# Row sums of the mixing weights: from products with a matrix of ones to adding transfers in DRAM

## The chip, the cores and the metric

One Trainium2 chip, one of its cores. The metric is the device time of one execution in microseconds (us). The kernel before takes 894.17 us, the median of three runs (894.03 to 894.5).

## The reference

One layer on a sequence of 1024 tokens with 1024 channels. An input projection feeds two branches, attention and a gated MLP that mixes positions inside blocks of 128; the gated branches are summed, projected and added to the input. What matters here is the mixing:

```python
def chunked_spatial_gating(u, v, w_s, b_s, ln_g, ln_b):
    v = layernorm(v, ln_g, ln_b)
    vb = v.reshape(B, nb, SG_BLOCK, SG_GROUPS, SG_GROUP_WIDTH)
    mask = cidx[None, :] <= cidx[:, None]          # chunks of 64
    w = jnp.where(mask[None], w_s, 0)
    mixed = jnp.einsum('gij,bnjgc->bnigc', w, vb) + transpose(b_s)[None, None, :, :, None]
    return u * mixed.reshape(B, S, SG_WIDTH)
```

The gain `ln_g` and offset `ln_b` belong to a channel and the mixing sums over positions `j`, so the offset can be taken out of the sum: the mixed value is `ln_g * (w @ normalized v)` plus `ln_b` times the sum over `j` of `w[g, i, j]`, plus `b_s`. Those sums, 8 groups by 128 positions `i`, so 1024 numbers, are the row sums of this case. They are needed on all 128 partitions, because a partition holds a channel there.

## The kernel before, in words

All matmuls work on pairs of float32r parts: `split` (L169) makes a high part with a cast on ScalarE (L176) and a low part with a subtraction on VectorE (L177); the tiles have the tags `wh` and `wl`, three buffers each. A large product is done by seven partial products of quadrant sums (forms b11, t1, t2, b21, t3, b22, t4), each of them 12 matmuls on 512 columns.

The stage of the change has three stretches.

1. `late_product` (L1005) runs three times, for the forms t2, t3 and t4 of the MLP's values: two halves `c`, four token tiles `t` each, six matmuls for every step (L793). After each step `pace[0]` is its last matmul. After every odd `t` one of the prepared `early` transfers is issued (`part_of_early`): these are DRAM to DRAM transfers of 512 KB (L316) on the queue of GpSimd, which make weight sums that are first read at 557 us. `paced` makes a transfer wait for `pace[0]`.
2. Between the second and the third `late_product` stand four matmuls with a matrix of ones (L1059): the row sums come out of them, on all partitions, in two PSUM banks `ps_sc`. In front of them the masked mixing weights `mix_w` (tag `wT`, its masked quarter set to zero at L1046) are split like all other weights (L1048).
3. `gemm_pair` (L371) makes two rows of the U projection at a time, four times over (L1146). In each call seven products follow one another, with a `hook` after each. Here the hook is `both` (L1131): one early transfer, and then two items of the list `late`: eight `statistics_of`, `normalize`, `bias_of(0)`, and then the mixes that the `finish` functions append. With two items a hook, the first two mixes stand behind the sixth product of the first pair and the next two behind the seventh.

`bias_of` (L1092) works out bias + row sum * `ln_b` with four VectorE instructions for four groups (L1101). `mix` (L1108) does the mixing matmuls (L1112) into one of two PSUM banks `ps_tp`, scales and adds the bias (L1120), multiplies the U tile by the result (L1128) and stores it to `s1_dr` through SyncE's queue (L520). U tiles have the tag `x`, five buffers.

The order on each engine comes from a scheduler that takes, of the instructions that its model holds ready, the one that stands first in the program; `after(second, first)` forces an order on one engine without a wait, and a `Sync` dependency makes a real wait. Queues run in order: an instruction of SyncE or GpSimd that waits holds all that are behind it. Weight loads go through `copy_to` (L212) on SyncE.

Of the kernel before, what the change touches and what calls it, by code (L numbers as in the profile page):

```python
# [24 lines left out]
F32 = mybir.dt.float32  # L25
F32R = mybir.dt.float32r
AF = mybir.ActivationFunctionType
ALU = mybir.AluOpType
PSUM = bass.MemoryType.PSUM

P = 128
D = 1024
S = 1024
KC = D // P
HALF = 512
# [17 lines left out]
def hybrid_tile(  # L53
# [16 lines left out]
    nc = tc.nc  # L70
# [8 lines left out]
    def nm(s):  # L79
        count[0] += 1  # L80
        return f"{s}_{count[0]}"

    def bank(tag, dt=F32):
        return psum.tile([P, 512], dt, name=nm("ps_" + tag), tag="ps_" + tag, bufs=2)

    def mtile(shape, dt, tag, bufs, pool=None):
        return (pool or main).tile(shape, dt, name=nm(tag), tag=tag, bufs=bufs)

    def scratch(name, shape=(D, S)):
        return dram.tile(list(shape), F32, name=name)  # L90
# [4 lines left out]
    def xtile():  # L95
        return mtile([P, HALF], F32, "x", 5)


    def after(second, first):

        tc.add_manual_dep(
            second.ins,
            first.ins.name,
            mybir.DependencyInfo(mybir.DependencyClass.NoSync, mybir.DependencyReason.DATA),
            reason="order",
        )
# [6 lines left out]
    ident = const.tile([P, P], F32, name="ident")  # L113
# [15 lines left out]
    lb_sb = const.tile([P, KC], F32, name="lb_sb")  # L129
# [5 lines left out]
    k_dr = scratch("k_dr", (P, 4, S))  # L135
    v_dr = scratch("v_dr", (NT, P, 2, 3 * HD))
    s1_dr = scratch("s1_dr")
    z_dr = scratch("z_dr")
    gs_dr = scratch("gs_dr")
    ga_dr = scratch("ga_dr")  # L140
# [28 lines left out]
    def split(hi, lo, src, minus=False):  # L169
        if minus:  # L170
            hi_of.append(nc.scalar.mul(hi, src, -1.0))
            return nc.vector.scalar_tensor_tensor(
                lo, src, -1.0, hi.bitcast(F32), op0=ALU.mult, op1=ALU.subtract
            )
        else:
            hi_of.append(nc.scalar.copy(hi, src))  # L176
            lo_of.append(nc.vector.tensor_sub(lo, src, hi.bitcast(F32)))  # L177
            return lo_of[-1]
# [73 lines left out]
    def half_of(half):  # L252
        return slice(half * HALF, (half + 1) * HALF)
# [46 lines left out]
    def paced(move):  # L300

        if pace[0] is not None:
            tc.add_manual_dep(
                move.ins,
                pace[0].ins.name,
                mybir.DependencyInfo(mybir.DependencyClass.Sync, mybir.DependencyReason.DATA),
                reason="pace",
            )
# [41 lines left out]
    term = [None]  # L350
# [3 lines left out]
    def product(acc, part, form, fresh, last=True):  # L354
        wh, wl = part
        bh, bl = form
        for k in range(4):
            ks = slice(k * P, (k + 1) * P)
            for n, (lt, rt) in enumerate(
                ((wh[:, ks], bh[:, k, :]), (wh[:, ks], bl[:, k, :]), (wl[:, ks], bh[:, k, :]))  # L360
            ):
                nc.tensor.matmul(  # L362
                    acc,
                    lt,
                    rt,
                    start=fresh and k == 0 and n == 0,
                    stop=k == 3 and n == 2,
                    skip_group_check=True,
                )

    def gemm_pair(b, finish, hook=lambda: None, second="o"):  # L371

        n = done[0]
        done[0] += 1
        acc = bank("mm")[:]
        x11, x12, x22 = xtile(), xtile(), xtile()
        product(acc, ready[n, 0], b["b11"], True)
        pace[0] = nc.scalar.copy(x11[:], acc)  # L380
        hook()
        t5 = bank("o")[:]
        product(t5, ready[n, 2], b["t1"], True)
        pace[0] = nc.scalar.mul(x22[:], t5, -1.0)
        hook()
        product(acc, ready[n, 3], b["t2"], False)
        pace[0] = nc.scalar.copy(x12[:], acc)
        split_next()
        hook()
        t2 = bank(second)[:]  # L390
        product(t2, ready[n, 1], b["b21"], True)
        term[0] = term_of_x11[0] = nc.vector.tensor_add(x11[:], x11[:], t2)
        finish(0, 0, x11, x11[:], 1.0)
        split_next()
        hook()
        product(acc, ready[n, 4], b["t3"], False)
        term[0] = nc.vector.tensor_sub(x22[:], x22[:], acc)  # L397
        finish(1, 1, x22, x22[:], 1.0)
        hook()
        product(t5, ready[n, 5], b["b22"], False)  # L400
        term[0] = nc.vector.tensor_add(x12[:], x12[:], t5)
        finish(0, 1, x12, x12[:], 1.0)
        split_next()
        hook()
        product(acc, ready[n, 6], b["t4"], False)
        finish(1, 0, xtile(), acc, -1.0)
        split_next()
        hook()
# [102 lines left out]
    def part_of_early(every=2):  # L511
        hooks[0] += 1
        if early and hooks[0] % every == 0:
            early.pop(0)()
# [28 lines left out]
    pool = outer.enter_context(tc.tile_pool(name="mixing", bufs=1))  # L543
# [71 lines left out]
    casts, lows, turns, scalings, squares = [], [], [], [], []  # L615

    def add_on(dst, src):
        return nc.gpsimd.dma_start(dst, src, accum_op=ALU.add)
# [127 lines left out]
    def pair_of_w():  # L746
        return mtile([P, D], F32R, "wh", 3), mtile([P, D], F32R, "wl", 3)
# [220 lines left out]
    mix_w = mtile([P, KC, P], F32, "wT", 1, pool)  # L968
# [23 lines left out]
    def statistics(t, half):  # L992
        return nc.vector.bn_stats(stats[:, t, half, :], xh[:, t, half_of(half)])
# [5 lines left out]
            for i in range(2):  # L999
                after(statistics(t + i, 0), lows[-1])  # L1000

    ones = mtile([P, P], F32R, "ones", 1, pool)
    after(nc.vector.tensor_scalar(ones[:], ident[:], 0.0, 1.0, op0=ALU.mult, op1=ALU.add), lows[-1])

    def late_product(name, weight, done, aside):  # L1005
        for c in range(2):
            for t in range(4):
                pace[0] = vs_product(accs[t], name, t, weight, False, cs=(c,))
                if t % 2:
                    part_of_early(1)  # L1010
                if c:
                    done(t)
                if aside:
                    aside.pop(0)()
# [26 lines left out]
        + [lambda t=t: part_of("t3", t) for t in range(4)]  # L1041
        + [lambda: gelu_of(0), lambda: gelu_of(2)],
    )
    row_sums = [bank("sc") for half in range(2)]
    split_w("s3", 1)
    after(nc.vector.memset(mix_w[64:128, :, 0:64], 0.0), lows[-1])  # L1046
    wh, wl = pair_of_w()
    split(wh[:], wl[:], mix_w[:].rearrange("p g i -> p (g i)"))  # L1048
    late_product(
        "t3",  # L1050
        "s3",
# [2 lines left out]
        + [lambda t=t: part_of("t4", t) for t in range(4)]  # L1054
        + [lambda: split_w("a22", 0, a22[0][:]), lambda: gelu_of(4), lambda: gelu_of(6)],
    )
    for half in range(2):
        for n, part in enumerate((wh, wl)):
            nc.tensor.matmul(row_sums[half][:], ones[:], part[:, half_of(half)], start=n == 0, stop=n == 1)  # L1059
    split_w("a22", 1, a22[1][:])  # L1060
    part_of_early(1)
    begin_job()
# [8 lines left out]
    late = []  # L1071
    in_twos = set()

    def hook():
        if len(late) == 1 and late[0] in in_twos:
            return
        for _ in range(2):
            if late:
                late.pop(0)()

    def statistics_of(t):
        statistics(t, 1)
        nc.vector.bn_aggr(mv[:, t, :], stats[:, t])
# [8 lines left out]
    def bias_of(half):  # L1092

        wT = mix_w[:, half * 4 : half * 4 + 4, :]
        bg = first_bias
        if half:
            bg = mtile([P, 4, P], F32, "bias", 1, pool)
            nc.sync.dma_start(bg[:].rearrange("p g i -> p (g i)"), sg_b[half_of(half)].partition_broadcast(P))
        for gg in range(4):
            g = half * 4 + gg  # L1100
            nc.vector.scalar_tensor_tensor(  # L1101
                bg[:, gg, :], row_sums[half][:, gg * P : (gg + 1) * P], lb_sb[:, g : g + 1], bg[:, gg, :], op0=ALU.mult, op1=ALU.add
            )
        return bg, wT

# [25 lines left out]
    def both():  # L1131
        part_of_early(1)
        hook()

    late.extend(lambda t=t: statistics_of(t) for t in range(NT))
    late.append(normalize)
    for m in range(0, KC, 2):

        def finish(i, half, q, src, sign, m=m):
            nc.scalar.activation(q[:], src, AF.Gelu, scale=sign)  # L1140
            late.append(lambda: mix(m + i, half, q))
            in_twos.add(late[-1])

        if m % 4 == 0:
            late.append(lambda m=m: bias.append(bias_of(m // 4)))
        gemm_pair(hb, finish, both)  # L1146
    while late:
        late.pop(0)()
# [5 lines left out]
    pool = stage.enter_context(tc.tile_pool(name="keys", bufs=1))  # L1154
# [44 lines left out]
    pool = stage.enter_context(tc.tile_pool(name="queries", bufs=1))  # L1199
# [210 lines left out]
    pool = stage.enter_context(tc.tile_pool(name="attention", bufs=1))  # L1410
# [234 lines left out]
    pool = stage.enter_context(tc.tile_pool(name="later", bufs=1))  # L1645
# [384 lines left out]
    for p in range(4):  # L2030
        n, t, acc, x11 = N_PAIRS + p, T_ORDER[p], accs[p], firsts[p]
# [93 lines left out]
        for e in range(2):  # L2125
            cs = slice(e * wide, (e + 1) * wide)
            part = bank("sc")[:, 0:wide]
# [95 lines left out]
```

## Time and profile before

| | |
|---|---|
| median of three runs | 894.17 us |
| the profiled execution | 894.7 us |
| its span | 892.9 us |
| PE busy in the span | 881.7 us, 99% |
| VectorE busy | 684.9 us, 77% |
| ScalarE busy | 580.1 us, 65% |
| GpSimd busy | 150.9 us, 17% |
| DMA, read and written | 146.37 MB and 86.11 MB |

The profile shows one execution on the one core. Times in a row of the timeline are the start and the duration in us, counted from the span's start; the rest of the row is engine, line of the kernel, operation, and written tile `<-` read tiles. An arrow in brackets names what ended the engine's idle time before the row.

### The profile page before, as it was taken

The page shows a single profiled execution, that of the slowest core. Times are in us where ns is not written, and L with a number is a line of the kernel's source. Part 1 is how long each engine was busy: PE and PEld are TensorE (multiplying, and loading weights), DVE is VectorE, ACT ScalarE, POOL GpSimd, SP SyncE. Part 2 cuts the span into 40 slices and gives each one's busy share as a digit, 9 for nine tenths or more (in the row PEclk, how much of TensorE's full clock was granted, in tenths as well). Part 3 has the DMA queues.
Part 4 walks back from the last instruction along what each step waited for, and adds up shares of the span by engine and source line. Part 5 has one row for each costly group of instructions (what it writes and reads, how often), then busy time and mean ns, then how long its engine had stood idle before and what let it go on. Part 6 is the DMA issues. An engine that isn't in the chain of part 4 may idle for free.

```text
span 892.9 us, 13164 instructions
## 1 busy us (share of the span) xinstructions
PE 881.7 (99%) x4117; PEld 731.4 (82%) x4117; DVE 684.9 (77%) x1362; ACT 580.1 (65%) x1189; POOL 150.9 (17%) x217
## 2 busy tenths in 40 slices
PE   8999999999999999999999999999999999999996
PEld 6888888888888888888888888888888888888885
DVE  7979966566686778888878888847796578579886
ACT  6875533334445489989989899955685385467443
POOL 3322222203030001111211011101121121110012
PEclk9999999999999999999999999999999999999999
DMA  9998888958778667888786789989899789998533
GB/s 332 211 268 222 268 206 172 176 153 265 250 252 286 214 189 189 210 185 195 179 236 210 237 225 222 250 290 383 308 289 376 276 231 258 298 307 282 179 119 118
DMA packets 131410, 212.40 MB, mean 238 GB/s; under 512 B 12778, under 2 KB 59882, under 8 KB 131340
## 3 DMA queue, kind: packets, MB, share of 16 engines
q1 hardware_dynamic: 108808, 148.62, 50.0%
q0 software_dynamic: 22384, 62.67, 31.6%
q8 instruction: 33, 0.54, 0.2%
q14 instruction: 37, 0.30, 0.1%
q10 hardware_dynamic: 148, 0.27, 0.1%
HBM read 146.37 MB, written 86.11 MB: 260 GB/s over the span
## 4 chain that ended last, share of the span: by engine, by line
PE 92%; ACT 3%; DVE 2%; issue 1%; DMA 1%; POOL 0%; SPq 0%; ACTq 0%; DVEq 0%
PE ps_mm L362 42%; PE ps_o L362 24%; PE ps_tp L362 7%; PE ps_sc L362 3%; PE ps_tp L793 2%; PE ps_o L793 2%; PE ps_mm L793 2%; PE ps_tp L1515 2%; PE ps_sc L1442 2%; PE ps_tp L1112 2%; PE ps_o L1550 1%; PE ps_sc L793 1%; ACT wh L176 1%; DVE wl L177 1%; PE ps_o L1555 1%
## 5 line engine op out<-in xcount | busy, mean ns | idle before, releaser
L176 ACT CAST wh<-s 128x1024 fp32r<-128x1024 f32 (+1 forms) x79 | 79.4, 1006 | 75.2 <-PE ps_mm L362 23.5
L177 DVE TENSOR_TENSOR wl<-wr,wh 128x512 fp32r<-128x512 f32 (+1 forms) x77 | 72.0, 937 | 58.0 <-ACT wh L176 57.9
L177 DVE TENSOR_TENSOR wl<-s,wh 128x1024 fp32r<-128x1024 f32 (+1 forms) x79 | 92.9, 1176 | 11.8 <-ACT wh L176 11.7
L176 ACT CAST wh<-wr 128x512 fp32r<-128x512 f32 (+1 forms) x77 | 63.0, 819 | 55.9 <-PE ps_mm L362 31.5
L1448 ACT COPY sl<-ps_sc 128x384 f32<-128x384 f32 (+2 forms) x128 | 51.8, 456 | 9.9 <-DVE sm L1454 9.9
L362 PE MATMUL ps_o<-T_t1h,wh 128*128 128x512 f32 x148 | 57.9, 391 | 0.0
L362 PE MATMUL ps_o<-T_t1h,wl 128*128 128x512 f32 x148 | 57.7, 390 | 0.0
L362 PE MATMUL ps_o<-T_t1l,wh 128*128 128x512 f32 x148 | 57.6, 389 | 0.0
L1470 ACT ACTIVATE pr<-pr,sm 128x192 f32<-128x192 f32 (+2 forms) x128 | 56.2, 444 | 0.1
L1454 DVE CUSTOM_DVE_ANT_0 pr<-sl,nsink_sb 128x192 f32<-128x192 f32 (+2 forms) x128 | 48.0, 399 | 9.9 <-ACT sl L1448 8.8
L362 PE MATMUL ps_mm<-T_b11h,wh 128*128 128x512 f32 x140 | 54.9, 392 | 0.0
L362 PE MATMUL ps_mm<-T_t3h,wh 128*128 128x512 f32 x140 | 54.7, 390 | 0.0
L362 PE MATMUL ps_mm<-T_b11l,wh 128*128 128x512 f32 x140 | 54.6, 390 | 0.0
L362 PE MATMUL ps_mm<-T_t2h,wh 128*128 128x512 f32 x140 | 54.6, 390 | 0.0
L362 PE MATMUL ps_mm<-T_b11h,wl 128*128 128x512 f32 x140 | 54.6, 390 | 0.0
L362 PE MATMUL ps_mm<-T_t3h,wl 128*128 128x512 f32 x140 | 54.6, 390 | 0.0
L362 PE MATMUL ps_mm<-T_t2l,wh 128*128 128x512 f32 x140 | 54.6, 390 | 0.0
L362 PE MATMUL ps_mm<-T_t3l,wh 128*128 128x512 f32 x140 | 54.5, 390 | 0.0
L362 PE MATMUL ps_mm<-T_t2h,wl 128*128 128x512 f32 x140 | 54.5, 389 | 0.0
L362 PE MATMUL ps_mm<-T_t4h,wh 128*128 128x512 f32 x136 | 53.2, 391 | 0.3 <-DVE x L397 0.3
L362 PE MATMUL ps_mm<-T_t4h,wl 128*128 128x512 f32 x136 | 53.0, 390 | 0.0
L362 PE MATMUL ps_mm<-T_t4l,wh 128*128 128x512 f32 x136 | 52.9, 389 | 0.0
(432 smaller groups left out, 2448.5 us busy)
## 6 DMA issues: line engine op xcount, KB each, us to landing
wr<-in_w_dram SPq DMA_DIRECT2D x86, 256.0 KB
sums<-in_w_dram POOLq DMA_DIRECT2D x20, 512.0 KB, 7.0
s<-sums SPq DMA_DIRECT2D x20, 512.0 KB
q_hl<-qhl SPq DMA_DIRECT2D x16, 512.0 KB
q<-q_hl SPq DMA_DIRECT2D x64, 128.0 KB
y_dr<-x POOLq DMA_DIRECT2D x28, 256.0 KB, 6.8
g<-in_w_dram POOLq DMA_DIRECT2D x12, 512.0 KB, 6.8
wr<-in_w_dram SPq DMA_DIRECT2D x11, 512.0 KB
```

The lines of the kernel that those rows point to most:

```text
L176: hi_of.append(nc.scalar.copy(hi, src))
L177: lo_of.append(nc.vector.tensor_sub(lo, src, hi.bitcast(F32)))
L362: nc.tensor.matmul(acc, lt, rt, start=fresh and k == 0 and n == 0, stop=k == 3 and n == 2, skip_group_check=True,)
L793: mm = nc.tensor.matmul(acc[:], lt, rt, start=fresh and k == 0 and n == 0, stop=stops and k == 3 and n == terms[-1], skip_group_check=True,)
L1112: nc.tensor.matmul(pm[:, t * P : (t + 1) * P], xh[:, half * 4 + t, g * P : (g + 1) * P], bias[-1][1][:, g % 4, :], start=True, stop=True,)
L1442: nc.tensor.matmul(sc, q_of[:, c, i * P : (i + 1) * P], kt[:, :, lo:hi], start=True, stop=True)
L1448: copies.append(nc.scalar.copy(two, sc))
L1454: nc.vector.tensor_tensor_reduce(v, two[:, 0, :], two[:, 1, :], 1.0, nsk[:, i : i + 1], op0=ALU.add, op1=ALU.min, accum_out=nmax[:, c, i : ...
L1470: e = nc.scalar.activation(v, v, AF.Exp, bias=nmax[:, c, i : i + 1], scale=-1.0, accum_out=sums[:, c, i : i + 1])
L1515: nc.tensor.transpose(dst, pr[:, i, block * P : block * P + width], ident[:])
L1550: nc.tensor.matmul(po[:, first], va[1][:, vs], a[:, n, first], start=n == 0, stop=n == 1, skip_group_check=True)
L1555: nc.tensor.matmul(po[:, cs], vb[c][:, vs], b[c][:], start=t == 0, stop=True, skip_group_check=True)
```

## The change

The split of `mix_w`, the matrix of ones, the four matmuls and their two PSUM banks go. `mix_w` and its masked quarter stay, since the mixes read them. Instead a DRAM scratch `rs_dr` of 64 rows by 1024 is made:

- `first_rows` copies rows 0 to 63 of the weights (`j` as the row) into it, 256 KB, on SyncE's queue;
- `second_rows` adds rows 64 to 127 where the mask lets them through: 64 rows, 8 groups, runs of 64 numbers, on GpSimd's queue;
- `add_rows(n)` adds the lower `n` of the first `2n` rows onto the upper ones, for n = 32, 16, 8, 4, 2, 1;
- `load_row_sums(half)` loads half of row 0 into all 128 partitions of a tile `rs` (one buffer), on SyncE's queue.

All are `paced`. The steps take even `t` of the three `late_product` runs: `first_rows`, `second_rows`, and then every second place `add_rows(32)` to `add_rows(2)`. `add_rows(1)` and `load_row_sums(0)` become items of `late`, so that `normalize`, `bias_of(0)` and the mixes of the first pair come one hook later. `bias_of` now reads `rs` in SBUF instead of PSUM, and its four instructions are ordered behind the last addition of a product (`term[0]`).

```diff
+    rs_dr = scratch("rs_dr", (64, D))
...
-    ones = mtile([P, P], F32R, "ones", 1, pool)
-    after(nc.vector.tensor_scalar(ones[:], ident[:], 0.0, 1.0, op0=ALU.mult, op1=ALU.add), lows[-1])
+    def add_rows(n):
+        return lambda: paced(nc.gpsimd.dma_start(rs_dr[0:n], rs_dr[n : 2 * n], accum_op=ALU.add))
+
+    def first_rows():
+        paced(nc.sync.dma_start(rs_dr[:], sg_w[0:64].rearrange("j g i -> j (g i)")))
+
+    def second_rows():
+        paced(add_on(rs_dr[:].rearrange("j (g i) -> j g i", g=KC)[:, :, 64:P], sg_w[64:P, :, 64:P]))
+
+    def load_row_sums(half):
+        row_sums.append(mtile([P, HALF], F32, "rs", 1, pool))
+        paced(nc.sync.dma_start(row_sums[half][:], rs_dr[0][half_of(half)].partition_broadcast(P)))
+
+    row_sums = []
+    adding = [first_rows, second_rows]
+    for n in (32, 16, 8, 4, 2):
+        adding += [None, add_rows(n)]
...
                 if t % 2:
                     part_of_early(1)
+                elif adding:
+                    step = adding.pop(0)
+                    if step is not None:
+                        step()
...
-    row_sums = [bank("sc") for half in range(2)]
...
-    wh, wl = pair_of_w()
-    split(wh[:], wl[:], mix_w[:].rearrange("p g i -> p (g i)"))
...
-    for half in range(2):
-        for n, part in enumerate((wh, wl)):
-            nc.tensor.matmul(row_sums[half][:], ones[:], part[:, half_of(half)], start=n == 0, stop=n == 1)
...
-            nc.vector.scalar_tensor_tensor(
-                bg[:, gg, :], row_sums[half][:, gg * P : (gg + 1) * P], lb_sb[:, g : g + 1], bg[:, gg, :], op0=ALU.mult, op1=ALU.add
+            after(
+                nc.vector.scalar_tensor_tensor(
+                    bg[:, gg, :],
+                    row_sums[half][:, gg * P : (gg + 1) * P],
+                    lb_sb[:, g : g + 1],
+                    bg[:, gg, :],
+                    op0=ALU.mult,
+                    op1=ALU.add,
+                ),
+                term[0],
             )
...
+    late.append(add_rows(1))
     late.extend(lambda t=t: statistics_of(t) for t in range(NT))
+    late.insert(8, lambda: load_row_sums(0))
     late.append(normalize)
...
+        if m == 2:
+            late.append(lambda: load_row_sums(1))
```

More of the change, by code (lines that the diff above doesn't have):

```diff
@@ L1133, in both @@
         hook()
+    assert not adding
+    late.append(add_rows(1))
     late.extend(lambda t=t: statistics_of(t) for t in range(NT))
+    late.insert(8, lambda: load_row_sums(0))
     late.append(normalize)
```

## The prediction

> **What bounds the kernel now.** First the engines' shares on the page, then busy time by stretch around the change, then the chain that ended last.
>
> ```profile
> PE 881.7 (99%) x4117; PEld 731.4 (82%) x4117; DVE 684.9 (77%) x1362; ACT 580.1 (65%) x1189; POOL 150.9 (17%) x217
> ```
> ```profile
> core 0: us, PE busy (x) PEld busy (x) DVE busy (x) ACT busy (x) POOL busy (x), PEclk, DMA share, GB/s
> 50.00:82.20 32.20, 32.20 (x143) 26.64 (x142) 26.80 (x40) 22.50 (x32) 7.16 (x10) 1.00 0.93 233
> 83.40:110.00 26.60, 26.60 (x119) 22.04 (x118) 24.84 (x49) 14.06 (x19) 7.38 (x13) 1.00 0.87 267
> 305.00:450.00 145.00, 144.00 (x706) 120.52 (x705) 119.32 (x349) 127.98 (x365) 20.94 (x25) 1.00 0.79 195
> 450.00:610.00 160.00, 158.90 (x767) 132.24 (x767) 123.89 (x329) 135.94 (x350) 20.40 (x29) 1.00 0.82 244
> ```
> ```profile
> 79.89 2.72 PE ps_tp L793 x12
> 82.61 0.93 PE ps_sc L1059 x4
> 83.55 2.72 PE ps_mm L793 x12
> ...
> 108.03 2.73 PE ps_o L362 x12
> 110.75 1.78 PE ps_tp L1112 x16
> 112.54 2.78 PE ps_mm L362 x12
> 115.31 1.78 PE ps_tp L1112 x16
> 117.10 2.75 PE ps_mm L362 x12
> ```
>
> PE is the bound: full clock, no idle time in the stretches from 50 to 110 us, and the chain runs from matmul to matmul. The four products with ones stand on it for 0.93 us. The other thing to see is the DMA share of 0.93 and 0.87 in just those stretches: the new transfers go into engines that are nearly full.
>
> **What is removed.** On PE four matmuls, 0.93 us by the chain (0.23 us each; a product of 12 takes 2.72 us, the same rate). PE is busy on both sides without a gap, so this comes off whole: -0.93 us. On the other engines:
>
> ```profile
> 59.01 0.22 DVE L1003 TENSOR_SCALAR ones<-ident 128x128 fp32r<-128x128 f32 x1
> 74.43 1.04 ACT L176 CAST wh<-wT 128x1024 fp32r<-128x1024 f32 x1
> 75.92 1.22 DVE L177 TENSOR_TENSOR wl<-wT,wh 128x1024 fp32r<-128x1024 f32 x1
> ```
>
> 1.04 us of ScalarE and 1.44 us of VectorE go at a place where PE never waited for either, so I count them, and the freed pair of `wh` and `wl` buffers, at nothing: the weights merely get ready earlier. What is late next there is PE's own queue.
>
> **What is added: the chain of adds.** `first_rows`, `second_rows`, six adds and a load, each reading what the one before wrote, so each waits for its landing. Their places: `first_rows` behind the first step of the t2 run (the t2 and t3 runs are 8 x 2.72 = 21.8 us long and end at 82.6, so they begin at 60.8; 60.8 + 1.36 = 62.2 us), `second_rows` at 64.9, then adds at 70.4, 75.8, 81.3, 86.7 and 92.2 (four steps apart, 2 x 2.72 = 5.44 us; after 82.6 less 0.93), the last behind the first `x` copy of the pair. The nearest rows for their price:
>
> ```profile
> sums<-in_w_dram POOLq DMA_DIRECT2D x8, 512.0 KB, 6.9
> ```
> ```profile
> sums<-in_w_dram POOLq DMA_DIRECT2D x1, 512.0 KB, 4.1
> ```
> ```profile
> sums<-in_w_dram POOLq DMA_DIRECT2D x20, 256.0 KB, 8.3
> k_dr<-qhl POOLq DMA_DIRECT2D x16, 32.0 KB, 3.1
> ```
> ```profile
> 83.61 1.05 ACT L176 CAST wh<-wr 128x1024 fp32r<-128x1024 f32 x1
> ...
> 102.97 0.58 ACT L387 COPY x<-ps_mm 128x512 f32<-128x512 f32 x1
> ...
> 122.61 0.60 ACT L384 ACTIVATE x<-ps_o 128x512 f32<-128x512 f32 x1 [2.13 <-PE ps_o L362]
> 125.15 0.62 ACT L176 CAST wh<-wr 128x512 fp32r<-128x512 f32 x1 [1.94 <-PE ps_mm L362]
> 127.82 1.05 ACT L176 CAST wh<-wr 128x1024 fp32r<-128x1024 f32 x1 [1.57 <-PE ps_o L362]
> ```
> ```profile
> 111.08 0.68 DVE L401 TENSOR_TENSOR x<-x,ps_o 128x512 f32<-128x512 f32 x1
> 111.68 1.23 DVE L177 TENSOR_TENSOR wl<-s,wh 128x1024 fp32r<-128x1024 f32 x1
> 112.82 1.41 DVE L1120 SCALAR_TENSOR_TENSOR ps_tp<-ps_tp,lg_sb,bias 128x512 f32<-128x512 f32 x2
> 114.14 1.27 DVE L1128 TENSOR_TENSOR x<-x,ps_tp 128x512 f32<-128x512 f32 x2
> ...
> 145.11 1.12 DVE L1101 SCALAR_TENSOR_TENSOR bias<-ps_sc,lb_sb,bias 128x128 f32<-128x128 f32 x4 [2.42 <-DMA bias<-in_sg_b_dram]
> ```
> ```profile
> 104.23 0.80 SPq L212 DMA_DIRECT2D wr<-in_w_dram  x2
> 114.84 5.50 SPq L520 DMA_DIRECT2D s_dr<-x  x4
> 141.54 0.33 SPq L1098 DMA_DIRECT2D bias<-in_sg_b_dram  x1
> ...
> 557.48 1.23 SPq L212 DMA_DIRECT2D s<-sums  x2
> ```
>
> The DMA rows end with the median time from issue to landing: 6.9 us for the eight early transfers between 62 and 83 us, 4.1 us for the one issued at 100.8 us, 8.3 us for accumulating transfers of 256 KB, 3.1 us for small ones of 32 KB. No row shows a small DRAM accumulate in a full queue, so one add (T) lies between 3.1 and 8.3 us. I take 5.5: an add stands 1.36 us behind a 512 KB early transfer of the same queue that needs 6.9, so it lands about when that does, 6.9 - 1.36 = 5.5 us after its own issue; the 128 KB to 4 KB of its own are little. `second_rows` I take at 8.3, the dearest row, issued at 66 us (an estimate: `first_rows` lands 3.6 us after 62.2, like the load of the bias, which was issued at 141.54 and released VectorE at 145.11). It lands at 74.3; six adds in line bring 74.3 + 6 x 5.5 = 107.3; the load of half of row 0, repeated over the partitions like that of the bias, costs 3.6: the row sums are there at Z = 110.9 us. With T = 3.1 the places set the time: the load waits for the copy that ends at 103.55 - 0.93 = 102.6, so Z = 106.2. With T = 8.3, Z = 127.7.
>
> **When Z would cost something.** VectorE reads the row sums behind the addition of L401, which now ends at 111.76 - 0.93 = 110.8. From Z on: four bias instructions 1.12, two of L1120 1.41, the first of L1128 0.64, so the first mix's bank is free at Z + 3.2. PE needs that bank for the third mix. The mixes come one hook later: b22 ends at 110.75 - 0.93 = 109.8, t4 112.6, two mixes 114.4, b11 of the next pair 117.1, and there the third mix starts. So Z is free up to 113.9, costs one for one beyond, eats the gain at 114.8, and passes +0.2% at 116.6. By my Z of 110.9 the cost is 0, with 3 us of cover: the products between. That is T of 6.0, 6.15 and 6.45.
>
> **The other moved parts.** On GpSimd early transfers stand behind each waiting add; nothing reads their sums before 557 us. On SyncE `first_rows` holds the first weight loads of the pairs until 62.2, and their first cast is at 83.6; `load_row_sums(0)` holds the loads issued at 104.23, whose first cast comes at 127.8, and the stores of the mixes, which come at 116.7 (PE start of the first mix 112.6 plus the 4.1 between 110.75 and 114.84). Both queues are free by Z - 3.6 = 107.3. The stores free `x` buffers for the next pair: 116.7 and, taking the 4.1 to 8.3 us of the rows above, 120.8 to 125.0, against the copy at 122.61 - 0.93 = 121.7. ScalarE idles 1.94 us behind that copy and PE needs the x12 copy that follows only before t3, so some 3.5 us of delay are covered; 0, at worst a few tenths. `load_row_sums(1)` waits for nothing late: its sums are wanted at 145. The extra traffic, about 1.1 MB (256 + 128 + 252 + 512 KB), is 4.5 us of DMA at 250 GB/s; no load of this stretch is on PE's path.
>
> **Sum.** -0.93 + 0 = -0.93 us. Against the profiled execution, 894.7 us with its span of 892.9, that is 893.8 and 892.0; the median of the runs stands 0.5 below that execution, and from it, 894.17, the forecast is 893.2 us. A change of 0.2%, 1.8 us, is about what a measurement can tell from none, so this counts as the same.
>
> [...] The row gives 3.1 us for 32 KB and 8.3 for an accumulate of 256 KB. [...]
>
> **Rivals.**
>
> 1. *The chain comes late.* Each add waits behind the early transfers, and VectorE stands at the bias. For it: the DMA shares above and the 8.3 us row; against it: while GpSimd waits it issues no early transfers, and those from 86 us on land faster (4.1 us by 100.8). It decides from T = 6.15. Midway, at T = 6.8: Z = 118.7, stall 4.8, less 0.93: 898.0 us. At its end, T = 8.3: stall 13.8, 907.0 us.
> 2. *`second_rows` is slow by its form.* It moves 512 runs of 256 bytes; the trace has no accumulate in such runs, so 8.3 may be short. At twice that, 16.6, the rest as forecast: Z = 119.2, stall 5.3, 898.5 us. Only half of such a delay fits in the cover. [...]
> 3. *Faster beyond the four matmuls.* The scheduler lays out later stages anew. PE idles 1.0 us and 1.1 us in the two attention stretches of the table; half of these 2.1 us would give -2.0 and 892.2 us. Nothing in the profile speaks for that direction: those waits don't come from this stage.
> 4. *The change doesn't shorten PE* because something else held it there: PE shows no wait at 82 us, so I leave it inside the forecast's band (894.2, the same verdict).
>
> **Chances.** Forecast, with rival 4: 0.63 (892.8 to 894.3). Late chain: 0.20, since T needs to be only a tenth over my 5.5. `second_rows`: 0.05. Faster: 0.12. So faster 0.12, same 0.63, slower 0.25. The range runs from the faster case, 892.2, to the middle of the late one, 898.0; beyond lie about 0.06 below and 0.12 above.
>
> **What the profile after would show.** The chain passes from L793 to L793 at 82.6 without L1059. The adds on GpSimd's row each wait for the one before; `add_rows(1)` is issued near 102 us and the load on SyncE near 107. VectorE shows a wait for `rs` of at most a few us before four L1101-like rows, and PE none at 117. If the adds are later than 6.15 us apart, PE waits before the third mix, and the forecast is wrong by that wait.

## The result, and the profile after

The changed kernel takes 905.41 us (median of six runs, 902.24 to 908.25) against 894.29 us for six of the kernel before (893.72 to 895.34): a ratio of 1.0122, 95% interval 1.0107 to 1.0138. It is slower by 1.2%; the forecast was 893.2 us with a range up to 898.0.

The profiled execution is the shortest of the six, 902.24 us. Its page, and then from the summary of waits the rows of PE and VectorE that weren't there before (columns: who waits, for whom, us in total, times, longest):

```profile
span 900.3 us, 13176 instructions
PE 882.0 (98%) x4113; PEld 732.6 (81%) x4113; DVE 683.6 (76%) x1360; ACT 579.2 (64%) x1188; POOL 157.9 (18%) x224
PEclk9999989999999999999999999999999999999999
```
```profile
DVE bias L1116 <- DMA rs<-rs_dr: 8.4, 1, 8.4
PE ps_tp L1134 <- DVE x L1150: 7.3, 1, 7.3
```

PE's busy time is what it was, 882.0 against 881.7, though four matmuls are gone; the span is 7.4 us longer; and one of the 40 digits of the clock has fallen. (The edit moves lines: L1101 is now L1116, L1112 L1134, L1120 L1142, L1128 L1150.) The chain that ended last shows the place:

```profile
109.30 8.16 DMA rs<-rs_dr
117.47 0.02 issue
117.49 0.07 DVE bias L1116
117.56 0.20 issue
117.76 0.14 DVE wl L178
...
119.77 1.14 DVE wl L178
120.91 1.33 DVE ps_tp L1142 x2
122.23 0.60 DVE x L1150
122.83 0.14 issue
122.96 3.75 PE ps_tp L1134 x16
126.72 2.89 PE ps_o L363 x12
```

The load of the repeated row sums leaves SyncE at 109.30 and releases VectorE only at 117.49, 8.2 us later. VectorE then works through the bias, two splits of weights that the scheduler put among and behind the four bias instructions, and the first two mixes, and frees the bank at 122.83. PE had finished its products at 115.7 and waited 7.26 us for that bank. The mixes that follow take 3.75 us instead of the 1.78 of before. Busy time by stretch says why (columns as in the prediction; the third number from the end is the granted clock, 1.00 at full rate):

```profile
114.00:115.00 1.00, 1.00 (x6) 0.82 (x5) 0.00 (x0) 0.00 (x0) 0.00 (x0) 1.00 1.00 334
118.00:122.80 4.80, 0.00 (x0) 0.00 (x0) 4.80 (x9) 0.00 (x0) 0.00 (x0) 0.72 0.71 205
124.00:126.00 2.00, 2.00 (x11) 2.00 (x11) 0.92 (x2) 0.00 (x0) 0.00 (x0) 0.50 0.54 202
128.00:131.00 3.00, 3.00 (x15) 2.49 (x14) 0.31 (x1) 0.60 (x1) 0.46 (x1) 1.00 0.25 95
```

While PE stood, its granted clock fell to half (0.72 on the mean from 118 to 122.8, 0.50 from there to 126), and PE worked at half for some 4 us after it went on (0.54 from 126 to 127, 1.00 from 128). So the profiled execution adds up: four matmuls off -0.93, PE's wait +7.26, slow mixes +1.97 (3.75 - 1.78), slow first product +0.17 (2.89 - 2.72), and -1.38 from the start, where this execution was ahead before the change could act (the run of 48 matmuls in front of the stage begins at 48.54 us, before at 49.92). That is +7.1 of the 7.4 us. The other five executions took 903 to 908 us and have no profile.

How the row sums came to be late: the issues on GpSimd's queue, then SyncE's issue of `first_rows`, then three landings:

```profile
68.43 1.06 POOL L619 DMA_DIRECT2D rs_dr<-in_sg_w_dram  x1 [5.18 <-DMA rs_dr<-in_sg_w_dram]
69.10 1.84 POOL L317 DMA_DIRECT2D sums<-in_w_dram  x2
72.84 0.83 POOL L1004 DMA_DIRECT2D rs_dr<-rs_dr  x1 [1.90 <-issue]
...
86.50 2.10 POOL L317 DMA_DIRECT2D sums<-in_w_dram  x3
89.89 0.83 POOL L1004 DMA_DIRECT2D rs_dr<-rs_dr  x1 [1.30 <-PE ps_mm L794]
90.44 1.34 POOL L317 DMA_DIRECT2D sums<-in_w_dram  x2
99.64 0.78 POOL L1004 DMA_DIRECT2D rs_dr<-rs_dr  x1 [7.86 <-DMA rs_dr<-rs_dr]
100.36 1.10 POOL L317 DMA_DIRECT2D sums<-in_w_dram  x2
102.33 0.80 POOL L1004 DMA_DIRECT2D rs_dr<-rs_dr  x1 [0.86 <-DMA rs_dr<-rs_dr]
102.99 2.70 POOL L317 DMA_DIRECT2D sums<-in_w_dram  x5
```
```profile
61.30 0.58 SPq L1007 DMA_DIRECT2D rs_dr<-in_sg_w_dram  x1
```
```profile
rs_dr<-rs_dr POOLq DMA_DIRECT2D x1, 16.0 KB, 9.2
rs_dr<-rs_dr POOLq DMA_DIRECT2D x1, 8.0 KB, 2.4
rs_dr<-rs_dr POOLq DMA_DIRECT2D x1, 4.0 KB, 6.8
```

While `second_rows` waited 5.18 us for `first_rows` to land, GpSimd issued nothing, and two early transfers followed right behind it at 69.10. The last three rows are the landings of the adds issued at 89.89, 99.64 and 102.33. Sizes don't order them: 16 KB took 9.2 us, 8 KB 2.4, 4 KB 6.8. What stood ahead in the queue does: three 512 KB transfers issued from 86.50 on in front of the first, nothing for some eight us in front of the second, two at 100.36 in front of the third. Each add lands just behind the last of them: by issue and time to landing, the last transfer in front lands at 98.9, 101.5 and 108.0 us, and the add at 99.1, 102.0 and 109.1. So the price of an add was the rest of the queue in front of it. And behind the last add stand five more at once, from 102.99; into those went the load of 109.30.

### The profile page after: what moved, and what is told of

The parts are those of the page before. It is cut to its first block, busy times and chain, and to the rows that moved or that the text cites. A ratio compares the mean times of both kernels' runs of the same rounds, so it can differ in the third digit from the quotient of the medians.

```text
span 900.3 us, 13176 instructions
## 1 busy us (share of the span) xinstructions
PE 882.0 (98%) x4113; PEld 732.6 (81%) x4113; DVE 683.6 (76%) x1360; ACT 579.2 (64%) x1188; POOL 157.9 (18%) x224
## 4 chain that ended last, share of the span: by engine, by line
PE 88%; DVE 4%; ACT 3%; DMA 2%; issue 2%; POOL 0%; SPq 0%; ACTq 0%; DVEq 0%
PE ps_mm L363 40%; PE ps_o L363 22%; PE ps_tp L363 7%; PE ps_sc L363 3%; PE ps_tp L794 2%; PE ps_o L794 2%; PE ps_mm L794 2%; PE ps_tp L1542 2%; PE ps_sc L1469 2%; PE ps_tp L1134 2%; PE ps_sc L794 1%; PE ps_o L1577 1%; DVE wl L178 1%; DMA rs<-rs_dr 1%; ACT wh L177 1%
## 5 line engine op out<-in xcount | busy, mean ns | idle before, releaser
L178 DVE TENSOR_TENSOR wl<-s,wh 128x1024 fp32r<-128x1024 f32 (+1 forms) x79 | 92.1, 1166 | 11.2 <-ACT wh L177 11.1
```

## The experiments

My theory after the result (A): all of the lost time is VectorE's wait for the row sums, handed to PE at the third mix, with the clock on top; and the row sums are late because the adds and the load share the DMA engines with 512 KB transfers in flight. Rivals: the shifted mixes (B), the added traffic and the waiting queues as such (C), the load's form, 128 times the same 2 KB just written (D).

### The load doesn't wait

```diff
-        paced(nc.sync.dma_start(row_sums[half][:], rs_dr[0][half_of(half)].partition_broadcast(P)))
+        paced(nc.sync.dma_start(row_sums[half][:], sg_w[0].rearrange("g i -> (g i)")[half_of(half)].partition_broadcast(P)))
```

> The changed kernel with all its transfers, but the load of the row sums reads one row of the weights instead of the sums, so it needn't wait for the last add (the row sums are wrong numbers here). Theory A (the time went to VectorE standing for the late row sums, and from there to PE at the third mix): the load is issued behind the copy at about 102 us and lands by 110, the wait of 8.4 us for rs and PE's gap of 7.3 us are gone, and 893.3 us, 0.93 under before. Rival C (the added traffic and the held queues cost, whatever the load reads): 898 us or more, PE still waits somewhere between 60 and 135 us.

Measured: 893.48 us, ratio to before 0.9989 (0.9980 to 0.9999). The order on PE, VectorE, ScalarE and GpSimd is the same as in the changed kernel, and the adds run later still (the last is issued at 108.89, there at 102.33); but VectorE goes from one instruction to the next without a wait, and PE loses 0.07 us between 110 and 135. The rows are VectorE's first reading of the row sums, the last add's issue, and PE's stretch:

```profile
110.53 0.35 DVE L1116 SCALAR_TENSOR_TENSOR bias<-rs,lb_sb,bias 128x128 f32<-128x128 f32 x1
```
```profile
108.89 0.80 POOL L1004 DMA_DIRECT2D rs_dr<-rs_dr  x1 [3.84 <-DMA rs_dr<-rs_dr]
```
```profile
110.00:135.00 25.00, 24.93 (x134) 21.15 (x133) 17.64 (x28) 7.60 (x12) 8.55 (x13) 1.00 1.00 273
```

So the first half of theory A holds: the wait is all of the loss, and what is left without it is the -0.9 us of the four matmuls. Why the row sums are late is not tested here.

### No adds at all

```diff
-    adding = [first_rows, second_rows]
-    for n in (32, 16, 8, 4, 2):
-        adding += [None, add_rows(n)]
+    adding = []
...
-    late.append(add_rows(1))
+    late.append(lambda: None)
```

(with the load of the run above)

> As the run with the ready load, and the eight transfers into and inside the DRAM scratch are left out too (row sums are wrong numbers). Theory A: the same 893.3 us within 0.7, since the adds cost nothing by themselves. Rival C: below the run with the ready load by a few us.

Measured: 893.23 us, 0.9988 (0.9979 to 0.9997). Within 0.3 us of the run with all adds: their traffic and their hold on GpSimd's queue cost nothing that can be measured. Rival C is out.

### The mixes a hook later, alone

```diff
+    late.append(lambda: None)
     late.extend(lambda t=t: statistics_of(t) for t in range(NT))
+    late.insert(8, lambda: None)
```

(in the kernel before)

> The kernel before with its products with ones, and two empty items in the list late, so that normalize, bias and the first mixes come a hook later as in the changed kernel. Theory A: nothing waits, 894.3 us within 0.9. Rival B (the mixes in their new places hold the x buffers and through ScalarE's copies PE): 897 us or more, with a wait of ScalarE's copy L384 for a store.

Measured: 894.29 us, 0.9997 (0.9987 to 1.0006). PE is busy from 110 to 135 us without a gap. Rival B is out.

### Early transfers held back from the first pair to the third

```diff
     def both():
-        part_of_early(1)
+        for _ in range((0, 1, 2, 1)[done[0] - 1 - first_pair]):
+            part_of_early(1)
         hook()
```

> The changed kernel, but the first pair issues no early transfers; those seven are issued in the third pair, two behind each product. Theory A with contention (the last add and the load are dear because five to six 512 KB transfers are in flight with them): the last add lands in about 3 us instead of 6.8, the load in about 4 instead of 8.2, the row sums are there some 8 us earlier, PE's gap goes, 893.5 us (893 to 895). Rival D (the load is dear by its form, 128 times the same 2 KB of DRAM that was just written): the load still takes about 8 us, only the last add is faster, PE waits some 3.5 us more than before and then runs slow for a while, 898 us.

Measured: 898.77 us, 1.0052 (1.0035 to 1.0069). The time is rival D's, the profile is theory A's. The last add, the load and VectorE's wait:

```profile
rs_dr<-rs_dr POOLq DMA_DIRECT2D x1, 4.0 KB, 2.7
```
```profile
106.64 0.33 SPq L1014 DMA_DIRECT2D rs<-rs_dr  x1
```
```profile
110.43 0.35 DVE L1116 SCALAR_TENSOR_TENSOR bias<-rs,lb_sb,bias 128x128 f32<-128x128 f32 x1 [0.92 <-DMA rs<-rs_dr]
```

The add takes 2.7 us and the same load 3.8, so rival D is out, and PE passes the third mix without a wait. The loss is in the third pair, where I had put the held transfers two behind each product:

```profile
156.40 16.76 DMA s_dr<-x
...
173.87 4.31 PE ps_mm L363 x12
178.18 2.10 PE ps_tp L1134 x16
```

A store of one mix needed 16.8 us to land among fourteen early transfers, its `x` buffer came free that late, ScalarE's copy waited 3.96 us for it and PE for the copy, 2.3 us; and then the product took 4.31 us instead of 2.73. This is the same fault at another place, made by my edit.

### The same seven, spread over the attention stage

```diff
     def both():
-        part_of_early(1)
+        if done[0] - 1 > first_pair:
+            part_of_early(1)
         hook()
...
         if not first:
-            part_of_early()
+            part_of_early(1 if of_pair[0] < 21 else 2)
```

> The changed kernel, the first pair issues no early transfers, and the seven are given back in the attention stage (from its 22nd hook on the hooks issue at each call, not at every second), where they stand apart. Theory A with contention: the last add in about 3 us, the load in about 4, row sums there near 110.5 us as in the run with seven held to the third pair, and now no store is held later: 893.3 us (892.8 to 894.3), a little under before. Rival (the third pair's wait of the last run was not from the transfers bunched there but from the changed order itself): 897 us or more, with a wait for a store between 135 and 180 us.

Measured: 894.9 us (892.62 to 897.13 in 12 runs), 1.0004 (0.9994 to 1.0013). The rival of a changed order is out: the profiled execution (892.89 us) waits neither for the row sums nor for a store; the load goes out at 104.83 and VectorE reads on at 109.09. But the median missed my 893.3 by 1.6 us. The row sums are there only just in time, and the spread suggests that some executions have them later; no profile of such a one was taken, so this is argued.

### The chain begun earlier

```diff
+    behind(nc.sync.dma_start(rs_dr[:], sg_w[0:64].rearrange("j g i -> j (g i)")), mm)
...
+    move = add_on(rs_dr[:].rearrange("j (g i) -> j g i", g=KC)[:, :, 64:P], sg_w[64:P, :, 64:P])
+    after(move, last_of_h)
...
-    adding = [first_rows, second_rows]
-    for n in (32, 16, 8, 4, 2):
-        adding += [None, add_rows(n)]
+    adding = []
+    for n in (32, 16, 8, 4, 2, 1):
+        adding += [add_rows(n), None]
```

> The changed kernel with the chain begun earlier: first_rows behind the load of the mixing weights (about 48 us), second_rows behind the last transfer of the forms (about 55), the six adds at the places from the first step of the t2 run on, the load in its old place. Theory A: the adds take what they took (4 to 10 us each), end near 95 us, the load goes out when its copy lets it, near 102, ahead of the bunch, and is there by 110: no wait for rs, 893.3 us (892.8 to 894.3). Rival D' (a load of just written DRAM is slow by its form): the load still takes 8 us, the row sums are there at 110, PE waits 0 to 1 us, 894.5 us.

Measured: 900.43 us, 1.0059 (1.0047 to 1.0071). A miss: begun 6 us earlier, the chain ended hardly earlier. First the issue of `first_rows` and `second_rows`, then the load from the chain:

```profile
54.95 0.58 SPq L973 DMA_DIRECT2D rs_dr<-in_sg_w_dram  x1
```
```profile
68.22 1.05 POOL L619 DMA_DIRECT2D rs_dr<-in_sg_w_dram  x1 [13.60 <-DMA rs_dr<-in_sg_w_dram]
```
```profile
106.56 9.83 DMA rs<-rs_dr
```

`first_rows` now needs 13.3 us (54.95 to 68.22) in a stretch with full DMA engines (GpSimd's queue has 51.5% of their time from 55 to 68 us and SyncE's 47.6%), so the head start is lost at the first step. GpSimd stood meanwhile, and its early transfers, held behind, came out later in a larger bunch: eight behind the last add, from 102.9 us, and the load took 9.8 us. The queues of that time, 102 to 117 us, with their share of the DMA engines:

```profile
q0 software_dynamic: 963, 3.38, 81.2%
q1 hardware_dynamic: 298, 0.56, 11.2%
```

q0 is GpSimd's, q1 SyncE's. The window begins 4.6 us ahead of the load. In the changed kernel, from the load's issue to its landing, 109.3 to 117.5 us, the shares are 82.4% and 19.5% (they count the time that packets took, here 101.9% together). So the load's queue had about a fifth of the engines' time there, and a ninth in the window of this run.

### The chain begun earlier, the mixes in their old places

```diff
-    late.append(lambda: None)
...
-    late.insert(8, lambda: load_row_sums(0))
+    load_row_sums(0)
```

(on the run above)

> As the run with the earlier chain, and the load is issued at the end of the t4 run instead of in the first pair's fifth hook, with no empty item in the list, so that the first mixes stand where they stood before the change. Theory A: the load goes out near 93 to 100 us and lands by 104; the first mixes read the bias at about 112; 893.3 us (892.8 to 894.3). Rival B (the places of the mixes matter): some tenths off the run with the earlier chain, in either direction.

Measured: 901.56 us, 1.0073 (1.0058 to 1.0089). Also a miss, for the same reason: the last add is issued at 102.21, the load goes out at 104.54 into eight early transfers and takes 10.5 us; PE waits 7.8 us at the mixes. With that wait in it the run says nothing of rival B.

### One more add

```diff
-    late.append(add_rows(1))
+    late.append(lambda: [add_rows(1)() for _ in range(2)])
```

> The changed kernel with the last add done twice, so that the chain is one landing longer (the row sums are wrong numbers). Theory A: the row sums come 4 to 9 us later, PE stands that much longer at the third mix, 909 to 914 us. Rival (the added time is not from the chain's end): 905 us as the changed kernel.

Measured: 907.69 us, 1.0142 (1.0126 to 1.0158). The chain is 4.8 us longer, the load leaves at 115.47 instead of 109.30, and PE's wait goes from 7.3 to 11.3:

```profile
115.47 7.88 DMA rs<-rs_dr
```
```profile
PE ps_tp L1134 <- DVE x L1150: 11.3, 1, 11.3
```

In the profiled executions (907.23 against 902.24) the 5.0 us of time come from 4.0 us of more waiting, 0.7 us of more slow matmuls behind it (the first product takes 3.62 us, there 2.89) and a start that is later by 0.6 us (the run of 48 matmuls begins at 49.16): they add up to within 0.3 us, and the waiting costs one for one, as theory A wants. The median is 1.3 us under the expected range, and the times alone hardly tell this kernel from the changed one (905.27 to 908.69 against 902.24 to 908.25); the profiles do.

### Twelve early transfers held back

```diff
                 if t % 2:
-                    part_of_early(1)
+                    if name != "t4":
+                        part_of_early(1)
...
     split_w("a22", 1, a22[1][:])
-    part_of_early(1)
...
     def both():
-        part_of_early(1)
+        if done[0] - 1 > first_pair:
+            part_of_early(1)
         hook()
...
-            part_of_early()
+            part_of_early(1 if of_pair[0] < 33 else 2)
```

> The changed kernel, and twelve early transfers are given back in the attention stage: the seven of the first pair and the five of the t4 run and just before it. Theory (each add lands behind the 512 KB transfers issued ahead of it in its queue, and the load behind those in flight): the 16 KB add takes 3 to 4 us instead of 9.2, the next two 2.5 to 3 at their own places, the last near 96 us, the load goes out with its copy near 101 and is there by 106, four us before it is wanted, so that no execution waits: 893.3 us (892.6 to 894.0), 0.999 of before, and the spread is that of before. Rival (the chain is slow by itself, some 6 us an add): the load at 105 and 894.9 us as with seven held.

Measured: 893.49 us (892.56 to 895.47 in 11 runs) against 894.31, 0.9994 (0.9986 to 1.0003). The 16 KB add, still behind one early transfer, takes 4.9 us instead of the 3 to 4 expected. The adds with nothing ahead of them take 2.1 and 2.2 us (8 and 4 KB); the load leaves with its copy and VectorE doesn't wait:

```profile
rs_dr<-rs_dr POOLq DMA_DIRECT2D x1, 8.0 KB, 2.1
rs_dr<-rs_dr POOLq DMA_DIRECT2D x1, 4.0 KB, 2.2
```
```profile
101.47 0.33 SPq L1014 DMA_DIRECT2D rs<-rs_dr  x1
109.28 0.35 DVE L1116 SCALAR_TENSOR_TENSOR bias<-rs,lb_sb,bias 128x128 f32<-128x128 f32 x1
```

This is the change as it was meant, at the 893.3 us expected. The median is 0.8 us under before, about the four matmuls, but the interval includes no change.

### Only the five of the t4 run held back

```diff
                 if t % 2:
-                    part_of_early(1)
+                    if name != "t4":
+                        part_of_early(1)
...
     split_w("a22", 1, a22[1][:])
-    part_of_early(1)
...
-            part_of_early()
+            part_of_early(1 if of_pair[0] < 21 else 2)
```

> The changed kernel with only the five early transfers of the t4 run and just before it held back (given back in the attention stage); the first pair issues its seven as in the changed kernel. Theory: the last add lands near 99 us, the load goes out near 101 us, before the five that are issued together behind the copy at 103, and is there by 108: 893.3 us (892.6 to 894.5). If instead the bunch slows a load that was issued ahead of it: row sums at 110 to 113, PE waits 0 to 3 us, 894 to 898 us.

Measured: 894.16 us, 1.0006 (0.9991 to 1.0022), and eleven runs in two groups: six from 892.61 to 894.16, five from 895.42 to 898.52. The profiled one is the longest, 898.52:

```profile
104.13 9.56 DMA rs<-rs_dr
```

Here `first_rows` landed late (`second_rows` was issued at 71.83), the last add landed at 104.0 and the load left behind a bunch issued from 101.05 on, so it took 9.6 us and PE waited 3.0 at the third mix; the mixes then took 2.53 us and the next product 3.86, at a clock of 0.57 between 120 and 124. That the short runs are those whose load left ahead of the bunch fits, and so does the mean granted clock, 0.996 or 0.997 in each of the five long runs and 0.998 or 0.999 in each of the six short ones; but none of the short ones was profiled.

## Why the prediction was wrong

The sum for the removed work was right: -0.93 us, and the runs without the wait give -0.8 to -1.2. What was put at nothing was right too for the shifted mixes, the traffic and the held queues (894.29 and 893.23 us), and VectorE and ScalarE's freed time brought nothing. Rival 1, the chain too late, is what happened, at the place and through the bank that the prediction named; it had 0.20. But it came by other terms than I had set for it. Its criterion, adds more than 6.15 us apart, was not even met: from 72.84 to 109.30 they are 6.1 us apart, which by my sum would have cost 0.5 us against the 0.93 gained. Term by term, for the profiled execution:

| term | forecast, us | measured, us |
|---|---|---|
| `first_rows` lands, `second_rows` issued | 66 | 68.4 |
| `second_rows` to the first add | 8.3 | 4.4 |
| six adds | 33 | 36.5 |
| the load, issue to VectorE | 3.6 | 8.2 |
| row sums there (Z) | 110.9 | 117.5 |
| from Z to PE's third mix | 3.2 | 5.5 |
| PE wants the third mix | 117.1 | 115.7 |
| half clock after the wait | 0 | 2.1 |

In sum, the row sums came 6.6 us late (`first_rows` +2.4, `second_rows` -3.9, the adds +3.5, the load +4.6), the way from them to the bank was 2.3 us longer, and PE came 1.4 us earlier; less the 3.0 us of cover, that is the 7.3 us of waiting. No term makes it alone: with the load at 3.6 PE would still have stood 2.7 us. The last add was issued at 102.33 where the sum has 101.8, but by luck, since the errors ahead of it cancel.

*The load.* The step "the load of half of row 0, repeated over the partitions like that of the bias, costs 3.6" failed, by 4.6 us, the largest error. The row was the right kind of transfer at the wrong time: the bias load of 141.54 went into a quiet stretch (GpSimd's queue has 0.8% of the engines' time from 141.5 to 145.2). The trace of before had the rows for the right one, five early transfers issued together behind the copy L387, with a median landing of 9.9 us:

```profile
103.84 2.94 POOL L316 DMA_DIRECT2D sums<-in_w_dram  x5 [2.29 <-ACT x L387]
```
```profile
sums<-in_w_dram POOLq DMA_DIRECT2D x5, 512.0 KB, 9.9
```

I had used the 4.1 us of a transfer just ahead of them, at 100.8, as evidence that the queue would be light. With nothing of GpSimd's in flight the same load takes 3.8 us (early transfers held to the third pair), among the early transfers 7.9 to 10.5 (eight of them at 9.8 and 10.5). The same row of the bias had priced `first_rows`: 7.1 us (61.30 to 68.43) instead of 3.6.

*From Z to the bank.* The sum 1.12 + 1.41 + 0.64 took the bias, the two scalings and one product as back to back. Two splits of weights stand between, 1.22 us each; one was in the row I had quoted at 111.68, and I left it out.

*The wait's own price.* "Costs one for one beyond" left out the clock. PE's wait of 7.3 us cost 2.1 us more in slow matmuls, that of 2.3 us in the third pair 1.9 (4.31 - 2.73 and 2.10 - 1.78), that of 3.0 us with five held 1.9 (2.53 - 1.78 and 3.86 - 2.72). The price hardly follows the wait's length, since the half clock lasted differently long. The times at half are estimates from each stretch's length and mean granted clock, with the slow part taken at 0.50, as in the changed kernel. Behind the wait of 2.3 us it is 0.66 over the 4.0 us from 174 and 0.88 over the 3.0 us from 178, 3.4 us at half; behind that of 3.0 it is 0.57 over the 4.0 us from 120, between stretches at 1.00, again 3.4. In the changed kernel it is 0.72 over the 4.8 us of the table, 0.50 up to 126 and 0.54 over the next us: 6.8 us, of which 2.8 passed while PE stood and cost nothing. With one more add it is 0.73 over the 25 us from 110: 13.5 us at half.

*`second_rows`.* The rival of its 256-byte runs is out: 4.4 us to the first add, half of what I took. The doubling to 16.6 us in it was an assumption that no run shows.

*What spoke against the rival.* "While GpSimd waits it issues no early transfers" is true and was no comfort: they come out together when the add has landed, just ahead of the load.

*The adds by themselves.* With an empty queue an add took 2.1 and 2.2 us (8 and 4 KB, twelve held back) and 2.5 us (8 KB, five held back); otherwise up to 10.5 us for 16 KB (early transfers held to the third pair).

## What to carry to other kernels

Price a transfer by what is in flight when it goes out, not by its size or by a like transfer in a quiet place: here 16 KB took 2.3 to 10.5 us and one load 3.8 to 10.5. A chain of transfers, each waiting for the one before, must not share its queue with bulk transfers that nobody needs soon (905.41 us with them ahead, 893.49 with twelve held back); hold those back first, and spread them, since a bunch put elsewhere held a store for 16.8 us and cost PE 2.3 us of waiting and 1.9 us at half clock. And when a wait reaches PE, add the slow matmuls behind it, some 2 us here whether PE stood 2.3 or 7.3, and 2.9 after 11.3.

## What the runs showed of the hardware

Beside a full queue of GpSimd SyncE's queue had far less than half of the DMA engines' time: 19.5% against 82.4% while a load of 256 KB took 8.2 us (the changed kernel), 11.2% against 81.2% from 102 to 117 us, where the same load took 9.8 us (the chain begun earlier), and 24.6% against 79.6% from 141 to 158 us, at whose end a store was issued that took 16.8 us (early transfers in the third pair). During the load of the changed kernel GpSimd moved 2.10 MB in 579 packets and SyncE 0.52 MB in 278, so SyncE's packets were about half as big. But the counts aren't even either, and no run here shows what sets them.

In GpSimd's own queue a small add landed just behind the bulk in front of it: 4 to 16 KB took 2.1 to 2.5 us with an empty queue or one nearly so, 6.8 and 9.2 in the changed kernel behind two and three transfers of 512 KB. A plain copy of 256 KB inside DRAM (`first_rows`) took 7.1 us when issued at 61 us (the changed kernel) and 13.3 us when issued at 55 (the chain begun earlier).
